# A streaming SiLU-multiply on one core: the two DMA rings exchanged, and the first tile cut into 2 and 6 rows

## The chip, the cores and the metric

One core of one Trainium2 chip. The metric is device time in microseconds (us), the median over several executions; a profile of one execution gives the span, which is about 1.8 us shorter than the device time. Executions of one kernel mostly agree within 0.3%, and this document argues about 0.1% to 0.6%, so most experiments were run in five rounds, interleaved with the kernel before on the same chip. Each kernel has one profile.

## The reference

```python
# x: (32, 512, 2048) float32; result: (32, 512, 1024) float32
x1, x2 = x[..., :1024], x[..., 1024:]
return x1 * (1 / (1 + np.exp(-x1))) * x2
```

The input is 134.22 MB, the output 67.11 MB. Nothing is used twice, so the kernel is a stream: load, one SiLU on ACT (ScalarE), one multiply on DVE (VectorE), store.

## The kernel before

The 16384 rows are cut into 16 tiles of 128 partitions x 8 rows. There are two input buffers and two output buffers. SP (SyncE) issues the loads, ACT the stores. Each issuing engine has its own ring, the queue of its transfers; the 16 DMA engines of the core work on both. In the trace a full load is 128 packets of 64 KB, a full store 128 packets of 32 KB. A load has *landed* when ACT may start on it, in these traces about 1.6 us after its last packet ended. A tile is computed in four pieces of 2 rows. Only the last tile stores each piece by itself.

```python
    K = 8
    KC = 2
    # ... in_pool and out_pool: bufs=2 each; xv, ov: "(n p k) d -> n p k d"
    def load(i):
        xt = in_pool.tile([P, K, in_cols], dt, name="xt")
        nc.sync.dma_start(out=xt, in_=xv[i])                  # SP's ring
        loaded[i] = xt

    load(0)
    load(1)
    for i in range(n_tiles):
        xt = loaded.pop(i)
        last = i == n_tiles - 1
        ot = out_pool.tile([P, K, half], dt, name="ot")
        for c in range(0, K, KC):
            ce = c + KC
            nc.scalar.activation(out=ot[:, c:ce, :], in_=xt[:, c:ce, :half], func=Silu)
            nc.vector.tensor_mul(out=ot[:, c:ce, :], in0=ot[:, c:ce, :], in1=xt[:, c:ce, half:])
            if last:
                nc.scalar.dma_start(out=ov[i][:, c:ce, :], in_=ot[:, c:ce, :])
        if not last:
            nc.scalar.dma_start(out=ov[i], in_=ot)            # ACT's ring
        if i + 2 < n_tiles:
            load(i + 2)
```

(Long argument lists are shortened here.) The scheduler put ACT's work on the last tile in this order: three activations, three stores, the fourth activation, the fourth store.

Of the kernel before, what the change touches and what calls it, by code (L numbers as in the profile page):

```python
# [1 line left out]

# [4 lines left out]


@with_exitstack
def kernel(  # L10
    ctx: ExitStack,
    tc: tile.TileContext,
    x: bass.AP,
    out: bass.AP,
):





    nc = tc.nc
    P = nc.NUM_PARTITIONS

    x_flat = x.flatten_outer_dims()
    out_flat = out.flatten_outer_dims()
    num_rows, in_cols = x_flat.shape
    half = in_cols // 2
    dt = x_flat.dtype

    K = 8  # L30
    KC = 2
    n_tiles = num_rows // (P * K)
    assert n_tiles * P * K == num_rows

    in_pool = ctx.enter_context(tc.tile_pool(name="in_pool", bufs=2))
    out_pool = ctx.enter_context(tc.tile_pool(name="out_pool", bufs=2))

    xv = x_flat.rearrange("(n p k) d -> n p k d", p=P, k=K)
    ov = out_flat.rearrange("(n p k) d -> n p k d", p=P, k=K)

    loaded = {}

    def load(i):
        xt = in_pool.tile([P, K, in_cols], dt, name="xt")
        nc.sync.dma_start(out=xt, in_=xv[i])  # L45
        loaded[i] = xt

    load(0)
    load(1)
    for i in range(n_tiles):  # L50
        xt = loaded.pop(i)
        last = i == n_tiles - 1
        ot = out_pool.tile([P, K, half], dt, name="ot")
        for c in range(0, K, KC):
            ce = c + KC
            nc.scalar.activation(  # L56
                out=ot[:, c:ce, :],
                in_=xt[:, c:ce, :half],
                func=mybir.ActivationFunctionType.Silu,
            )  # L60
            nc.vector.tensor_mul(  # L61
                out=ot[:, c:ce, :],
                in0=ot[:, c:ce, :],
                in1=xt[:, c:ce, half:],
            )
            if last:
                nc.scalar.dma_start(out=ov[i][:, c:ce, :], in_=ot[:, c:ce, :])  # L67
        if not last:
            nc.scalar.dma_start(out=ov[i], in_=ot)
        if i + 2 < n_tiles:  # L70
            load(i + 2)


# [1 line left out]
_INS = ['x']  # L75
_OUTS = [((32, 512, 1024), 'float32')]


# [23 lines left out]
```

## Time and profile before

| | before |
|---|---|
| median time of the first three runs | 472.03 us (471.82 to 472.82) |
| span of the profiled run | 470.1 us |
| moved | 201.35 MB, mean 428 GB/s over the span |
| DVE busy, ACT busy | 142.4 us, 118.3 us |
| full tiles begin | every 29.02 us (mean of 13, 74.82 to 452.05 us) |
| last load landed; last store issued | 451.97 us; 465.37 us |

From the page of the kernel before: the busy tenths of the DMA engines in 40 equal slices of the span, then the gigabytes per second in the same slices, then the totals.

```profile
DMA  8999999999999999999999999999999999999998
GB/s 357 446 446 401 401 485 435 418 401 443 449 446 401 441 457 396 446 474 390 468 404 438 457 441 407 427 420 449 446 410 432 480 401 418 440 474 424 399 424 337
HBM read 134.22 MB, written 67.11 MB: 428 GB/s over the span
```

DMA is busy in every slice, the first and last a little less. A tile of 12.58 MB every 29.02 us is 434 GB/s. The Trainium skill, "DMA: Bandwidth & Descriptors", section "Where 436 GB/s comes from", gives 435.2 GB/s for the fabric; this trace sits on that figure.

The chain of waits of the same run, its share by line and its last pieces (start, duration, what):

```profile
by line: DMA xt<-in_x_dram 79.6%; DVE ot L61 15.2%; ACT ot L56 3.7%; issue 0.2%; SPq L45 0.1%; ACTq L67 0.1%; ACTq L56 0.0%
...
405.10 46.87 DMA xt<-in_x_dram
...
453.99 6.71 DVE ot L61 x3
...
460.72 0.34 ACTq L67
461.06 0.05 issue
461.11 1.92 ACT ot L56
463.02 0.02 issue
463.05 2.29 DVE ot L61
```

DVE's 15% are misleading: the chain goes through DVE because a load can be issued only when the multiply has freed its buffer, but the other load is in flight all that time and DMA doesn't stop. In the last tile it is different: no load is left to hide behind.

The end of the timeline (start, duration, engine, line, operation, count, and the idle time before it with what ended it; ACTq and SPq are the queues in which ACT and SP issue transfers):

```profile
452.05 5.51 ACT L56 ACTIVATE ot<-xt 128x2048 f32<-128x2048 f32 x3 [21.65 <-DMA xt<-in_x_dram]
453.99 6.70 DVE L61 TENSOR_TENSOR ot<-ot,xt 128x2048 f32<-128x2048 f32 x3 [20.06 <-ACT ot L56]
456.32 4.74 ACTq L67 DMA_DIRECT2D out_dram<-ot  x3
461.11 1.91 ACT L56 ACTIVATE ot<-xt 128x2048 f32<-128x2048 f32 x1 [3.54 <-DVE ot L61]
463.05 2.29 DVE L61 TENSOR_TENSOR ot<-ot,xt 128x2048 f32<-128x2048 f32 x1 [2.36 <-ACT ot L56]
465.37 0.34 ACTq L67 DMA_DIRECT2D out_dram<-ot  x1
```

ACT stands in its queue behind three stores, each of which waits for DVE; the fourth activation starts 3.54 us late.

The same stretch in windows of 1 us (window, length, DVE, ACT and POOL busy, clock, DMA share, GB/s):

```profile
457.00:458.00 1.00, 1.00 (x1) 0.56 (x1) 0.00 (x0) 1.00 0.54 229
458.00:459.00 1.00, 1.00 (x2) 0.00 (x0) 0.00 (x0) 1.00 0.93 393
464.00:465.00 1.00, 1.00 (x1) 0.00 (x0) 0.00 (x0) 1.00 0.95 401
465.00:466.00 1.00, 0.34 (x1) 0.00 (x0) 0.00 (x0) 1.00 0.24 98
466.00:467.00 1.00, 0.00 (x0) 0.00 (x0) 0.00 (x0) 1.00 0.94 393
```

A window counts a packet whole where it starts. The starts and durations of the packets in the trace show a hole of 1.0 us from 465.2 to 466.3, just before the last store.

### The profile page before, as it was taken

Reading aid. Unit: us, or ns where it says so; the run is one execution under the profiler, and the core shown is the slowest. Engines: PE = TensorE matmul, PEld = TensorE weight load, DVE = VectorE, ACT = ScalarE, POOL = GpSimd, SP = SyncE. Lnnn points to the kernel's source line nnn. Section 1 sums busy time; section 2 is a strip of 40 time slices with the busy share of each in tenths; the row PEclk is TensorE's granted clock in tenths of the full one; section 3 lists DMA queues with packets and bytes.
Section 4 is the critical chain, followed back from the end, with each engine's and each line's share of the span. In section 5 each row is a group of like instructions: output and inputs, shape, how many; then the busy total and the mean of one; then the engine's idle time right before and its main releaser. Section 6 shows DMA issues by size and latency. Waiting matters only on the chain.

```text
span 470.1 us, 267 instructions
## 1 busy us (share of the span) xinstructions
DVE 142.4 (30%) x64; ACT 118.3 (25%) x65; POOL 0.2 (0%) x4
## 2 busy tenths in 40 slices
DVE  0070704207052070511606115070250702407033
ACT  1050506014060240602306032060320604106041
POOL 0000000000000000000000000000000000000000
DMA  8999999999999999999999999999999999999998
GB/s 357 446 446 401 401 485 435 418 401 443 449 446 401 441 457 396 446 474 390 468 404 438 457 441 407 427 420 449 446 410 432 480 401 418 440 474 424 399 424 337
DMA packets 5042, 201.35 MB, mean 428 GB/s; under 512 B 560, under 2 KB 560, under 8 KB 560
## 3 DMA queue, kind: packets, MB, share of 16 engines
q1 hardware_dynamic: 2304, 134.22, 66.2%
q10 hardware_dynamic: 2736, 67.11, 33.1%
q14 instruction: 2, 0.02, 0.0%
HBM read 134.22 MB, written 67.11 MB: 428 GB/s over the span
## 4 chain that ended last, share of the span: by engine, by line
DMA 80%; DVE 15%; ACT 4%; issue 0%; ACTq 0%; SPq 0%
DMA xt<-in_x_dram 80%; DVE ot L61 15%; ACT ot L56 4%; SPq L45 0%; ACTq L67 0%; ACTq L56 0%
## 5 line engine op out<-in xcount | busy, mean ns | idle before, releaser
L61 DVE TENSOR_TENSOR ot<-ot,xt 128x2048 f32<-128x2048 f32 x64 | 142.4, 2286 | 322.9 <-ACT ot L56 322.9
L56 ACT ACTIVATE ot<-xt 128x2048 f32<-128x2048 f32 x64 | 117.1, 1898 | 344.0 <-DMA xt<-in_x_dram 340.4
L56 ACT ACT_TABLE_LOAD x1 | 1.3, 1283 | 0.7 <-PEq L86 0.7
L86 POOL MEMSET const-bfloat16-1.0<- 128x1 bf16 x1 | 0.1, 101 | 0.0
L86 POOL MEMSET const-uint8-127<- 128x1 uint8 x1 | 0.1, 101 | 0.0
L86 POOL MEMSET const-float32-0.0<- 128x1 f32 x1 | 0.1, 98 | 0.2 <-issue 0.2
L86 POOL MEMSET const-float32-1.0<- 128x1 f32 x1 | 0.1, 98 | 0.0
## 6 DMA issues: line engine op xcount, KB each, us to landing
out_dram<-ot ACTq DMA_DIRECT2D x15, 4096.0 KB, 39.7
out_dram<-ot ACTq DMA_DIRECT2D x4, 1024.0 KB, 5.4
xt<-in_x_dram SPq DMA_DIRECT2D x16, 47.1
```

Source lines behind the costliest of these rows:

```text
L56: nc.scalar.activation(out=ot[:, c:ce, :], in_=xt[:, c:ce, :half], func=mybir.ActivationFunctionType.Silu,)
L61: nc.vector.tensor_mul(out=ot[:, c:ce, :], in0=ot[:, c:ce, :], in1=xt[:, c:ce, half:],)
L86: nc = _bacc.Bacc("TRN2", target_bir_lowering=False, num_devices=1)
```

## The change

Its intent: let the first store start early, by making the first tile small, and free ACT from stores, by giving the loads to ACT and the stores to SP. The diff without its regrouping of the views:

```diff
-    n_tiles = num_rows // (P * K)
+    PLAN = [2, 6] + [K] * (num_rows // (P * K) - 1)
+    # plan: (first row, rows per partition) of each tile; view(flat, i): its slice
+    ctx.enter_context(tc.manual_schedule())
     def load(i):
         xt = in_pool.tile([P, K, in_cols], dt, name="xt")
-        nc.sync.dma_start(out=xt, in_=xv[i])
+        nc.scalar.dma_start(out=xt[:, :plan[i][1], :], in_=view(x_flat, i))
 ...
             if last:
-                nc.scalar.dma_start(out=ov[i][:, c:ce, :], in_=ot[:, c:ce, :])
+                nc.sync.dma_start(out=ov[:, c:ce, :], in_=ot[:, c:ce, :])
         if not last:
-            nc.scalar.dma_start(out=ov[i], in_=ot)
+            nc.sync.dma_start(out=ov, in_=ot[:, :k, :])
```

More of the change, by code (lines that the diff above doesn't have):

```diff
@@ L31, with view @@
     KC = 2
-    n_tiles = num_rows // (P * K)
-    assert n_tiles * P * K == num_rows
+    PLAN = [2, 6] + [K] * (num_rows // (P * K) - 1)
     in_pool = ctx.enter_context(tc.tile_pool(name="in_pool", bufs=2))
     out_pool = ctx.enter_context(tc.tile_pool(name="out_pool", bufs=2))
-    xv = x_flat.rearrange("(n p k) d -> n p k d", p=P, k=K)
-    ov = out_flat.rearrange("(n p k) d -> n p k d", p=P, k=K)
+    plan = []
+    row = 0
+    for k in PLAN:
+        plan.append((row, k))
+        row += P * k
+    assert row == num_rows
+    n_tiles = len(plan)
+    def view(flat, i):
+        row0, k = plan[i]
+        return flat[row0:row0 + P * k].rearrange("(p k) d -> p k d", k=k)
+    ctx.enter_context(tc.manual_schedule())
     loaded = {}
@@ L50 @@
     for i in range(n_tiles):
+        k = plan[i][1]
         xt = loaded.pop(i)
         last = i == n_tiles - 1
+        ov = view(out_flat, i)
         ot = out_pool.tile([P, K, half], dt, name="ot")
-        for c in range(0, K, KC):
-            ce = c + KC
+        for c in range(0, k, KC):
+            ce = min(c + KC, k)
             nc.scalar.activation(
```

## The prediction

> **What bounds it now.** The DMA engines: the slices of the span show them busy throughout, and the DMA line gives 201.35 MB at a mean 428 GB/s. The chain of waits is 80% loads of xt, 15% DVE, 4% ACT, but DVE (30% busy) and ACT (25%) are in it only because two input buffers tie each load to the computing of the tile two before; meanwhile the other load is in flight, so DMA never stops. By the timeline tiles start 28.97 us apart (74.82, 103.89 ... 452.05). A tile moves 12.58 MB: 434 GB/s. The Trainium skill, "DMA: Bandwidth & Descriptors", section "Where 436 GB/s comes from", gives a ceiling of 435.2 GB/s; the trace agrees. All bytes at 434 GB/s take 464 us of the span's 470.1. The other 6 us: 1.3 us before the first packet, some 2 us of holes around the last stores (DMA view, near 457.5 and 465.5), 1.4 us after the last packet, and slower small packets (3.15 MB in 7.6 us from 457.6 on, 414 GB/s).
>
> **What the change does.**
> 1. Rings exchanged: same bytes, same 16 engines. The same page, "Issuing engines are not separate DMA queues", says the issuer doesn't matter: 0 us. Loads now wait for DVE on ACT's queue, but ACT already waited there for its store, and its next activation needs a load landing some 18 us later.
> 2. In the last tile ACT no longer stops for stores: now the fourth activation waits 3.54 us for DVE (waits), and the last store is issued 13.4 us after the last landing (451.97 to 465.37). Without this, 0.06 + 1.92 + 4 x 2.29 = 11.1 us: 2.3 us earlier.
> 3. First tile of 2 rows: it lands near 8 us rather than 22.7; the first store starts near 12 us, not 33.6. This removes no idle time, as DMA is busy with loads from 1.3 us anyway; it only moves stores ahead of loads. By my bookkeeping of the two queues (alternate packets, 434 GB/s) about 0.5 MB more is stored when two old tiles are loaded, so the last load lands 1.2 us later (453.2), and less of the store before it is left to cover the last tile's first 4.2 us of computing. This gives back part of the 2.3 us.
> 4. The manual schedule: nothing more.
>
> Net: the last stores go out at DMA's pace, about 2.5 us each, behind a hole of about 1 us; the end comes 0.5 to 1.5 us sooner, all in the tail.
>
> **Predicted:** 471.2 us, 80% range 468.8 to 473.0. Faster by over 2% 0.01, within 2% 0.97, slower 0.02.
>
> **What would show it.** (a) Mean rate still about 429 GB/s, full tiles still 29.0 us apart. (b) No wait of ACT for DVE in the last tile; last store issued 11.1 us after the last landing. (c) First landing near 8 us, first store near 12, yet the last landing at 452 to 454.5. (d) A DMA hole of at most 2 us after the last load, none elsewhere.
>
> **What would make it wrong.** Exchanged rings served unequally; reads and writes mixed from 12 us on being slower than loads alone; packets of 8 to 24 KB costing more than I took; store backlog running dry, with an earlier last landing and longer tail, or stores all caught up and the last tile's computing exposed (up to 3 us slower).

## The result, and the profile after

| | before | after |
|---|---|---|
| median time | 472.16 us (4 runs) | 473.21 us (4 runs, 473.05 to 474.37) |
| ratio | | 1.0026, 95% interval 1.0006 to 1.0045 |
| span of the profiled run | 470.1 us | 471.3 us |
| last tile's first activation | 452.05 us | 454.63 us |
| last store issued after that | 13.3 us | 10.9 us |

A ratio is the mean time of one kernel's runs over that of the other's of the same rounds, so it is not quite the ratio of the medians. Executions over 1.5% slower than the fastest of the same kernel are left out of the means. The time is within 2%, as forecast, but on the other side: the forecast was 0.8 us less, the first measurement is 1.1 us more, 0.2 us outside the stated range.

From the page of the changed kernel, the DMA slices and totals:

```profile
DMA  9998999999999999899999999999999999999988
GB/s 374 393 479 371 437 438 445 464 389 473 409 439 442 445 409 470 387 434 445 473 409 445 409 437 448 406 446 459 398 434 439 439 448 445 406 437 423 434 356 356
HBM read 134.22 MB, written 67.11 MB: 427 GB/s over the span
```

The middle looks as before. The first two lines here are the beginning of its timeline, the others the end:

```profile
8.54 1.91 ACT L70 ACTIVATE ot<-xt 128x2048 f32<-128x2048 f32 x1 [5.63 <-DMA xt<-in_x_dram]
12.80 104.89 SPq L83 DMA_DIRECT2D out_dram<-ot  x5
...
454.63 7.31 ACT L70 ACTIVATE ot<-xt 128x2048 f32<-128x2048 f32 x4 [21.69 <-DMA xt<-in_x_dram]
456.57 8.90 DVE L75 TENSOR_TENSOR ot<-ot,xt 128x2048 f32<-128x2048 f32 x4 [20.10 <-ACT ot L70]
458.89 6.94 SPq L81 DMA_DIRECT2D out_dram<-ot  x4
```

The first store is indeed issued at 12.80 us instead of 33.62, and ACT indeed runs its four last activations without a stop. But the last tile begins 2.58 us later. The windows around its first and last stores show what that does (columns as before):

```profile
457.00:458.00 1.00, 1.00 (x1) 1.00 (x1) 0.00 (x0) 1.00 0.16 66
458.00:459.00 1.00, 1.00 (x2) 1.00 (x2) 0.00 (x0) 1.00 0.00 0
459.00:460.00 1.00, 1.00 (x1) 1.00 (x1) 0.00 (x0) 1.00 0.32 131
464.00:465.00 1.00, 1.00 (x1) 0.00 (x0) 0.00 (x0) 1.00 0.94 393
465.00:466.00 1.00, 0.47 (x1) 0.00 (x0) 0.00 (x0) 1.00 1.04 434
466.00:467.00 1.00, 0.00 (x0) 0.00 (x0) 0.00 (x0) 1.00 1.02 418
```

The hole before the last store is gone, and a larger one has come in front of the last tile's first store, 457.9 to 459.8 by the packets. DMA has nothing to do: the last load has landed, the store of the tile before is done, and the last tile's first piece is still in ACT and DVE.

The packet records allow an exact account. "Stored" is what the store packets had moved at the moment named; "idle" is the mean idle time of an engine from 400 us to the last packet.

| from the packets | before | after |
|---|---|---|
| first store packet | 39.5 us | 16.5 us |
| moved in all by 40 us | 15.82 MB | 15.82 MB |
| stored when load packets of 16.78 MB had ended | 0.79 MB | 2.55 MB |
| stored when load packets of 25.17 MB had ended | 4.99 MB | 6.09 MB |
| moved in all by 450 us | 193.67 MB | 193.68 MB |
| stored when the last load packet ended | 59.58 MB at 450.3 us | 60.78 MB at 453.0 us |
| idle at the end | 1.01 us | 1.93 us |

The two kernels move the same number of bytes: at every 5 us from 40 to 450 us the totals agree within 0.01 MB. What differs is which bytes: the changed kernel has 1.2 MB more stored and as much less loaded, so its last load comes later and fewer stores are left to cover the last tile's computing. (The early rows depend on how packets in flight are counted. With the loads in flight counted in proportion too, 1.49 against 2.68 MB are stored when 16.78 MB are loaded, again 1.2 MB more.)

What has to be covered is longer than the computing. In the changed kernel 6.7 us pass from the end of the last load packet (453.04) to the first store packet of the last tile (459.72): 1.6 us until the load has landed, 4.3 us of computing, 0.8 us from issue to packet. At that moment 2.1 MB of earlier stores were left (67.11 - 4.19 - 60.78), 4.9 us at 434 GB/s, so an estimate of the hole is 1.8 us; 1.84 was measured. In the kernel before 3.3 MB were left, 7.7 us, and there was no hole in that place.

### The profile page after: what moved, and what is told of

It is laid out like the page before. It is cut to its first block, busy times and chain, and to the rows that moved or that the text cites. A ratio compares the mean times of both kernels' runs of the same rounds, so it can differ in the third digit from the quotient of the medians.

```text
span 471.3 us, 275 instructions
## 1 busy us (share of the span) xinstructions
DVE 142.4 (30%) x64; ACT 118.3 (25%) x65; POOL 0.2 (0%) x4
## 3 DMA queue, kind: packets, MB, share of 16 engines
q1 hardware_dynamic: 2880, 67.11, 33.1%
HBM read 134.22 MB, written 67.11 MB: 427 GB/s over the span
## 4 chain that ended last, share of the span: by engine, by line
DMA 79%; DVE 15%; ACT 4%; DVEq 0%; issue 0%
DMA xt<-in_x_dram 79%; DVE ot L75 15%; ACT ot L70 4%; DVEq L111 0%
```

## The experiments

Eleven kernels were run, all correct, each in five rounds. The theory: **stores that start early take their place from loads; the last load comes later by what was stored extra; that by itself is free, but it uses up the store backlog that should cover the way from the last load to the last tile's first store, and the hole costs time.** The rivals: the exchange of rings itself costs; the small first loads cost; the small packets cost; or the first ratio was noise.

| kernel | last tile begins, us | span, us | median, us | ratio to before (95%) |
|---|---|---|---|---|
| before | 452.05 | 470.1 | 472.0 | 1 |
| after, first result | 454.63 | 471.3 | 473.21 | 1.0026 (1.0006 to 1.0045) |
| after_again | 454.30 | 470.9 | 472.93 | 1.0020 (1.0007 to 1.0032) |
| swap8 | 451.87 | 469.8 | 471.74 | 0.9993 (0.9980 to 1.0005) |
| split_oldrings | 454.68 | 472.9 | 474.67 | 1.0054 (1.0040 to 1.0068) |
| sp_tail_only | 452.52 | 470.3 | 472.02 | 0.9999 (0.9987 to 1.0011) |
| hold_store | 453.66 | 470.5 | 471.66 | 0.9994 (0.9982 to 1.0007) |
| hold_pad | 451.57 | 469.6 | 471.70 | 0.9989 (0.9977 to 1.0001) |
| late_store | 451.27 | 470.4 | 471.70 | 0.9991 (0.9978 to 1.0004) |
| tail_half | 454.21 | 470.2 | 471.94 | 1.0004 (0.9991 to 1.0016) |
| load_halves | 467.77 (its second half) | 479.3 | 491.89 | one fast run of six |
| warm_load | 452.04 | 470.1 | 471.84 | 0.9998 (0.9985 to 1.0010) |
| warm_store | 451.78 | 469.8 | 471.67 | 0.9994 (0.9980 to 1.0007) |

### swap8: the change without the split tile

```diff
-    PLAN = [2, 6] + [K] * (num_rows // (P * K) - 1)
+    PLAN = [K] * (num_rows // (P * K))
```

> The changed kernel with all sixteen tiles at 8 rows: rings exchanged, ACT unblocked in the last tile, first tile not split. Theory (the early small stores push the last load back, and the DMA hole it opens in front of the last tile's stores costs the time): the last load lands where it did before, 452.0 +- 0.4 us; no DMA hole in the tail, because the store of tile 14 lasts to about 457.6 and the first store of the last tile reaches DMA at about 457.1; span 469.4 against 470.1, that is 0.5 to 1.0 us faster than before (ratio near 0.998). Rival (the exchange of rings itself costs, loads on ACT's ring being served later): the last load lands near 454.6 as in the changed kernel, and the time is not better than before.

The last tile begins at 451.87, as before, and the span is 469.8 (expected 469.4). The exchange of rings does not delay the loads. The gain expected of at least 0.5 us was not seen: 0.3 us by the ratio, with 1 inside its interval.

### split_oldrings: the split tile alone, on the old rings

The kernel before with the plan of 2, 6, 8, ... rows and its scheduler's order, loads on SP and stores on ACT.

```diff
+    PLAN = [2, 6] + [K] * (num_rows // (P * K) - 1)
 ...
-        nc.sync.dma_start(out=xt, in_=xv[i])
+        nc.sync.dma_start(out=xt[:, :plan[i][1], :], in_=view(x_flat, i))
```

> The kernel before with the first tile split in 2 and 6 rows and nothing else: loads on SP, stores on ACT, the fourth activation of the last tile still waits for DVE. Theory: the last load lands at about 454.6, as in the changed kernel; two holes in the tail, 1.8 us before the first small store and about 1.5 us before the last; span about 472.6, 2 to 3 us slower than before (ratio near 1.005). Rival (ring exchange is what delays): last landing 452.0, span 470.1, ratio 1.000.

As expected: last tile at 454.68, and two holes. Its windows:

```profile
457.00:458.00 1.00, 1.00 (x1) 1.00 (x1) 0.00 (x0) 1.00 0.31 131
458.00:459.00 1.00, 1.00 (x2) 1.00 (x2) 0.00 (x0) 1.00 0.01 0
459.00:460.00 1.00, 1.00 (x1) 1.00 (x1) 0.00 (x0) 1.00 0.31 131
467.00:468.00 1.00, 0.97 (x1) 0.00 (x0) 0.00 (x0) 1.00 0.28 115
468.00:469.00 1.00, 0.00 (x0) 0.00 (x0) 0.00 (x0) 1.00 0.32 131
```

The first (1.7 us by the packets) is that of the changed kernel, the second (1.5 us) is the one that ACT's stop makes. The split alone costs 2.65 us (474.67 against 472.02). So the delay belongs to the split, whichever ring has the loads.

### sp_tail_only: freeing ACT in the last tile, and nothing else

```diff
-                nc.scalar.dma_start(out=ov[i][:, c:ce, :], in_=ot[:, c:ce, :])
+                nc.sync.dma_start(out=ov[i][:, c:ce, :], in_=ot[:, c:ce, :])
```

> The kernel before with one thing changed: the last tile's four stores are issued by SP, so ACT does not stop in the last tile; rings and tiles as before. Theory (the exchange of rings is worth nothing of itself; the freed ACT closes the hole of 1.0 us before the last store): last landing 451.5 to 452.2 us as before, the last store issued 11.1 us after it, no hole before it, span 469.1 to 469.9, the same as the kernel with rings exchanged and 8-row tiles (469.8) within 0.4 us. Rival (the ring exchange gave the small gain): span 470.1 as before.

ACT no longer stops and the hole before the last store is gone, but the last tile begins at 452.52 and the span is 470.3, both above the ranges expected, and the ratio is 0.9999. Closing a hole of 1.0 us gained nothing that can be measured. Part of the reason is in the packets. The packets of one engine follow one another end to start, so that the 16 engines can be told apart. In the kernel before they ended between 468.72 and 468.88 us: those that had fallen behind caught up during the hole, and all began the last store together. Here they ended between 467.79 and 469.05 us. Most finished earlier, the last one did not, and the last counts: an engine's mean idle time at the end fell only from 1.01 to 0.70 us. Swap8 looks the same (467.47 to 468.57, mean idle 0.80). The gain of 0.3 us there and of nothing here are within each other's intervals, so nothing is shown for the exchange of rings either.

### hold_store: the small loads kept, the early store taken away

The first eight rows of each partition are loaded as 2 and 6 rows, computed into one output tile and stored at once. (Shortened: the computing of the 6 rows writes to rows 2 to 7 of the output tile of the first part.)

```diff
+        if i < 2:   # in view(): both parts from one 8-row tile
+            first = flat[0:P * K].rearrange("(p k) d -> p k d", k=K)
+            return first[:, 0:2, :] if i == 0 else first[:, 2:K, :]
 ...
-        if not last:
+        if i == 1:
+            nc.sync.dma_start(out=whole, in_=ot)      # all 8 rows
+        elif i > 1 and not last:
             nc.sync.dma_start(out=ov, in_=ot[:, :k, :])
```

> The changed kernel with the loads of 2 and 6 rows kept, but no store until both parts are computed: one store of 8 rows (32 KB packets) as before, issued near 32 us. Theory: it is the early store, not the small loads, that delays the last load; so the last landing is back at 451.5 to 452.5 us, no hole in the tail, span about 469.4, 0.4 to 1.0 us faster than before. Rival (small first loads, or a third tile in flight, cost the delay): last landing near 454.6 and span near 471.3.

From its timeline:

```profile
31.24 0.36 SPq L89 DMA_DIRECT2D out_dram<-ot  x1
...
453.66 7.31 ACT L75 ACTIVATE ot<-xt 128x2048 f32<-128x2048 f32 x4 [21.69 <-DMA xt<-in_x_dram]
```

The time is back (0.9994), but the last tile begins at 453.66, later than expected, and a hole of 0.8 us is left (458.0 to 458.8 by the packets; the kernel before has one of 1.0 us in another place). Both theories missed the landing. The reason offered: when the second load lands only 6 rows are left to compute instead of 8, so the store is issued at 31.24 instead of 33.47 us (swap8), and its first packet is at 37.3 instead of 39.6. If the start of the first store decides, that should be undone by waiting 2.3 us. The next run does this.

### hold_pad: the same, with a needless copy ahead of the first store

```diff
+            nc.vector.tensor_copy(out=ot[:, 0:4, :], in_=ot[:, 0:4, :])
             nc.sync.dma_start(out=whole, in_=ot)
```

> The kernel with loads of 2 and 6 rows and one store for both, with one needless DVE copy (128x4096, 2 to 4.5 us) ahead of that store, so the first store packet moves from 37.3 us back to 39.5 or later. Theory (the start of the first store sets how far loads lag, for good: 2.3 us earlier made the last landing 1.8 us later): the last landing goes back from 453.7 to 450.5 to 452.3 us. Rival (small first loads cost something of their own): last landing stays near 453.5. Time: span 469.5 to 470.2, no hole.

The copy took 2.29 us. The beginning and the end of this run's timeline:

```profile
31.05 2.29 DVE L89 COPY ot<-ot 128x4096 f32<-128x4096 f32 x1
33.37 0.37 SPq L90 DMA_DIRECT2D out_dram<-ot  x1
...
451.57 7.31 ACT L75 ACTIVATE ot<-xt 128x2048 f32<-128x2048 f32 x4 [21.57 <-DMA xt<-in_x_dram]
```

The first store packet is at 39.5 and the last tile begins at 451.57, 2.1 us earlier than without the copy. (The two kernels ran on different chips, but in the five other kernels with a first store packet at 39.5 to 39.9 us it begins within 451.78 to 452.52, on both chips.) Useless work at 31 us moved a landing at 450 us forward, 14 tiles later. The small loads cost nothing that shows. The order of the first 45 us is carried almost unchanged to the end: in the kernel before, "stored" grows by 4.19 to 4.24 MB per tile loaded from the third tile on, and the 1.1 MB by which the changed kernel is ahead at the third tile are 1.2 MB at the end.

### late_store: the first store later than before

Swap8 with the same copy ahead of the first store only.

```diff
+        if i == 0:
+            nc.vector.tensor_copy(out=ot[:, 0:4, :], in_=ot[:, 0:4, :])
         if not last:
             nc.sync.dma_start(out=ov, in_=ot[:, :k, :])
```

> Rings exchanged, all tiles of 8 rows, and a needless DVE copy (128x4096, 2 to 4.5 us) ahead of the first store only. Theory: the last load lands earlier than the 451.9 of the kernel without the copy, by 1 to 3 us, yet the span stays at 469.8 +- 0.5: an earlier last landing wins nothing, because the backlog of stores is then longer and DMA is busy all the same; only a hole costs. Rival (the last landing sets the end, as the chain of waits has it): span 1 to 3 us shorter, 467 to 469.

The first store packet came at 42.2 us and the last tile began at 451.27, 0.6 us earlier than in swap8; 1 to 3 us were expected, so the landing moved less than thought. The time (0.9991) is that of swap8 (0.9993). The profiled execution was the slowest of the five; its span, 470.4, is 0.1 us above the range expected and far from the rival's 467 to 469. An earlier last landing wins nothing that these runs resolve; the step of 0.6 us is too small to say more.

### tail_half: the changed kernel with a smaller first piece in the last tile

```diff
-        for c in range(0, k, KC):
-            ce = min(c + KC, k)
+        cuts = [0, 1, 2, 4, 6, 8] if last else list(range(0, k + 1, KC))
+        for c, ce in zip(cuts, cuts[1:]):
```

> The changed kernel whole, only the last tile is cut in pieces of 1, 1, 2, 2, 2 rows and not 2, 2, 2, 2, so its first store is ready 2.1 us sooner. Theory: the last landing stays at 454.6, but the hole of 1.84 us before the first small store shrinks to under 0.3 us (another of up to 1 us may open after the half-size stores, since computing 8 rows takes 9.4 us after the first piece); span 469.4 to 470.5, 0.8 to 1.9 us less than the changed kernel's 471.3. Rival (the late landing as such, or slow small packets, cost the time and not the hole): span 471.3 or more.

The last tile still begins late, and the time falls by 1.0 to 1.3 us, from 472.93 and 473.21 (the two medians of the changed kernel) to 471.94. The start of the last tile, and its windows:

```profile
454.21 7.40 ACT L70 ACTIVATE ot<-xt 128x1024 f32<-128x1024 f32 x5 [21.65 <-DMA xt<-in_x_dram]
...
457.00:458.00 1.00, 0.66 (x1) 1.00 (x2) 0.00 (x0) 1.00 0.44 184
458.00:459.00 1.00, 0.95 (x1) 1.00 (x2) 0.00 (x0) 1.00 0.94 385
460.00:461.00 1.00, 1.00 (x2) 1.00 (x1) 0.00 (x0) 1.00 0.47 193
```

The window with nothing in it has gone; by the packets a hole of 0.75 us at 460.5 is left, behind the two half-size stores, where it was expected. So the loss of the changed kernel is the hole, not the late landing as such and not the small packets, of which this kernel has more.

### load_halves: load packets as small as store packets

Swap8 with each load issued as two of 4 rows, so that a packet of either ring is 32 KB.

```diff
-        nc.scalar.dma_start(out=xt[:, :plan[i][1], :], in_=view(x_flat, i))
+        nc.scalar.dma_start(out=xt[:, 0:4, :], in_=view(x_flat, i)[:, 0:4, :])
+        nc.scalar.dma_start(out=xt[:, 4:8, :], in_=view(x_flat, i)[:, 4:8, :])
```

> Rings exchanged, all tiles of 8 rows, each load issued as two of 4 rows, so that load packets are 32 KB like those of the stores. Theory (the two rings are served packet by packet): while both have work a store gets half of DMA and not a third, about 217 GB/s, so a full store's packets span about 18 us and not 25; the first store packet comes 3 to 4.5 us after its issue rather than 6.1; stores get ahead, the last load lands at 453.5 to 456 us, and the hole before the last tile's first store opens without any split first tile: 1.5 to 5 us, span 471 to 474. Rival (shares go by bytes, not packets): store span, last landing and time as with whole loads, 451.9 and 469.8.

Its mechanism came out: the packets of a full store spanned 18.7 to 20.7 us instead of 24.6 to 25.3 (swap8), and the first store packet came 4.65 us after its issue instead of 6.1. While both have packets the rings are served by turns, a packet each, whatever the packets' sizes. The size was far off: the last half tile landed at 467.77 us, because it shared DMA evenly with the store of tile 14, and by then all but a few late packets of the earlier stores had been written. Windows of the end:

```profile
460.00:465.00 5.00, 0.00 (x0) 0.00 (x0) 0.00 (x0) 1.00 0.93 393
465.00:469.00 4.00, 0.00 (x0) 1.23 (x1) 0.00 (x0) 1.00 0.05 20
469.00:473.00 4.00, 3.29 (x2) 2.48 (x2) 0.00 (x0) 1.00 0.12 51
473.00:478.00 5.00, 1.21 (x1) 0.00 (x0) 0.00 (x0) 1.00 0.95 395
```

That is the same hole at its full size, 8.0 us by the packets (464.9 to 472.9). In the first 1.2 us a few engines still load; the other 6.7 us are the whole way from the last load packet through its landing, ACT and DVE to the next store packet, as long as in the changed kernel, with hardly any backlog under it. Only one of six executions (481.07 us, the profiled one) counts as fast; the others, up to 498.39, are over 1.5% longer and are left unexplained.

### after_again

The changed kernel unaltered.

> The changed kernel unaltered, five rounds, beside the two kernels below. Theory: the first result holds, 1.0 to 1.5 us slower than before (ratio 1.002 to 1.003), last landing 454 to 455 us, one hole of 1.5 to 2.2 us before the last tile's first store. Rival (the first ratio was noise between runs): ratio 0.999 to 1.001.

Ratio 1.0020, hole from 458.1 to 459.4 us. The loss is real; noise is out. This median, 472.93, would have been just inside the predicted range, so the range was missed by a hair and the direction clearly.

### warm_load and warm_store: a side question

DMA loses about 1 us once, about the time that stores begin, in the nine kernels whose first tile is stored as a whole (in the four with a store of 2 rows first, load packets between 20 and 39 us take 0.5 to 0.7 us too long per engine in all). In the kernel before, 16 load packets that begin between 36 and 40 us, as many as there are engines, take about 1 us too long. Both kernels are swap8 with one tiny transfer on SP at the start, a load into an unused tile, or a store of zeros that the last tile overwrites.

```diff
     load(0)
+    nc.sync.dma_start(out=warm, in_=x_flat[0:P, 0:128])          # warm_load
     load(1)
+    nc.sync.dma_start(out=out_flat[num_rows - P:num_rows, 0:128], in_=warm)   # warm_store, instead
```

> Rings exchanged, all tiles of 8 rows, and SP first issues one tiny load (128x128) on the ring of the stores. In every run so far DMA loses about 1 us once, in the 4 us in which the first store packets begin (36 to 40 us in the kernel before, one load packet on each engine takes about 1 us too long). Theory A (it is a first use of that ring): the loss goes, span 468.9 to 469.2. Theory B (it is the first writing to HBM, or nothing of the ring): the loss stays, span 469.8, time 0.999 to 1.000 of before.

> As the tiny load, but a tiny store (128x128 zeros, overwritten by the last tile 450 us later) at the start. Theory A and theory C (first writing to HBM) both say that the 1 us loss goes, span 468.9 to 469.2; if it stays here and with the tiny load, it belongs to every change from pure loads to loads and stores mixed, span 469.8.

Spans 470.1 and 469.8, and by the packets the loss is still there (0.85 and 0.9 us). So neither a first use of the ring nor a first writing explains it. What it is stays open.

## Why the prediction was wrong

**What held.** DMA bounds the kernel, at 434 GB/s before and after; (a) the middle is unchanged. The exchange of rings is worth nothing that these runs resolve (swap8, sp_tail_only), as the prediction took from the Trainium skill, "DMA: Bandwidth & Descriptors", section "Issuing engines are not separate DMA queues". (b) ACT's stop vanished, with the last store issued 10.9 us after the last tile's first activation. (c) The first landing near 8 us (8.51) and the first store near 12 us (12.80). The mechanism of step 3 is right: the early store ends no idle time, it delays loads.

**The step that failed** is the size in step 3: "about 0.5 MB more is stored when two old tiles are loaded, so the last load lands 1.2 us later". Measured: 1.2 MB more when two old tiles are loaded with packets in flight counted in proportion (2.68 against 1.49; 1.76 by the table's count) and 1.2 MB more at the end (60.78 against 59.58), and the last tile begins 2.6 us later. (c)'s upper limit of 454.5 was just passed. From it follows the second size, the hole "of about 1 us", which was 1.84 us (within (d)'s 2 us).

Where the delay comes from, in two steps that were run (together 2.8 us counted from swap8, 2.6 from the kernel before): from swap8 to hold_store (only 6 rows left to compute when the second load lands, so the first store starts 2.3 us earlier) 1.8 us; from hold_store to the changed kernel (1 MB stored still earlier, by itself, and both first stores in smaller packets) 1.0 us. The prediction does not name the first of these as an effect of its own.

Why the bookkeeping was short stays open. Its rule, packets by turns, is what the traces show. When each DMA engine's packets are put in order, the kernel before alternates load and store, with one exception: between two transfers of one ring that are both queued, the ring misses one turn. From 46 to 440 us two loads follow each other 208 times (16 engines x 13 tiles), always after an engine's eighth store packet, the last of a store, and two stores 208 times, always after the eighth load packet. So the second store, issued at 56.76, has its first packet at 68.5, 3.9 us after the last of the store before. The changed kernel misses the same turns between stores in every tile, so they don't explain a difference between the two. The wait of the first store may be a part: it was 5.9 us from issue to first packet in the kernel before and 3.7 us in the changed one, and 2.2 us at a third of 434 GB/s are 0.3 MB (an estimate).

**A second error, in the value of freeing ACT.** The prediction counted "some 2 us of holes around the last stores", near 457.5 and 465.5. The one near 457.5 was no hole but an artefact of counting packets where they start (their starts and durations show 14 or more of the 16 engines busy throughout 457 to 459); only 1.0 us was there to win. And where it was closed alone (sp_tail_only) the time did not move. With the split tile the same freeing matters: it closes the second hole of split_oldrings, and the span falls from 472.9 to 471.3.

**The sum.** In the prediction, 2 us of holes gave way to one of 1 us, a gain. Measured, a hole of 1.0 us gave way to one of 1.84: an engine's mean idle time at the end rose from 1.01 to 1.93 us, which is 0.9 of the 1.1 us by which the span grew. Of the rest, 0.1 us lies after the last packet; 0.1 us was not pursued. The same count holds for the experiments: in all twelve profiles but that of load_halves, span less mean idle time at the end is 469.0 to 469.6 us, while the spans go from 469.6 to 472.9. The split costs 2.65 us alone; with ACT freed it costs 1.2 to 1.5 us (the changed kernel's 472.93 and 473.21 against swap8's 471.74); without it there is at most a small gain.

No version beats the kernel before clearly. The best ratio, 0.9989 for the kernel with the needless copy, has an upper limit of 1.0001. With all bytes at 434 GB/s taking 464 us, there was never more than about 1% to gain, if that rate is the limit.

## What to carry to other kernels

When DMA is busy without a break, as here, starting stores earlier does not shorten anything: it only exchanges loads for stores, and the last load comes later. Keep a backlog of stores for the end that is longer than the way from the last load packet to the first store packet of the last tile (6.7 us here, 2.9 MB at 434 GB/s), or make the last tile's first piece small. Judge a hole in DMA from the packets' starts and ends, not from a window that counts packets where they start, and remember that a hole also lets lagging engines catch up, so closing it can win less than its length.

## What the Trainium skill lacked or had wrong

- "DMA: Bandwidth & Descriptors", section "Queues, rings and completion order", says that each engine takes turns between its rings packet by packet. The order of the packets agrees, and so does the effect of their size (a store's packets span 18.7 to 20.7 us beside 32 KB load packets, 24.6 to 25.3 beside 64 KB). The page lacks that a ring misses one turn between two transfers that are both queued (208 times of 208 for either ring of the kernel before); over all engines the stores' ring pauses 3.7 to 4.0 us in each tile.
- The same page, section "Latency and other measured facts", gives about 600 ns to the first byte from the hardware queues. From the end of the issuing instruction, DMA being idle, it is 0.63 us for the first load (1.10 to 1.73) and 0.50 us for the last store of the kernel before (465.71 to 466.21), which agrees. The page lacks the wait beside a running stream of 64 KB load packets, 5.5 us for the first store (34.00 to 39.54).
- The same page, section "Where 436 GB/s comes from", says that for transfers between HBM and SBUF the HBM side (about 358) binds, and "HBM Reference", section "Specifications (TRN2)", gives about 425 GB/s for a core alone; loads and stores mixed ran at 434 GB/s here on the one core that was used.
- No page has the loss of about 1 us once, when full stores first join a stream of loads (0.95 us in the kernel before); neither a tiny load nor a tiny store at the start removes it (0.85 and 0.9 us).
- No page says how far the 16 engines drift apart in a stream without a hole; in the six kernels without one at the end their last packets ended 0.8 to 1.5 us apart (0.16 us apart after a hole, in the kernel before).
